# A hybrid retention/attention layer with a gated MLP: the up-projection by Strassen's algorithm, the output projection by token halves, and the late stages in program order

## The chip, the cores and the metric

The kernel runs on one core of one Trainium2 chip, in one launch. The metric is the device time of the whole launch in microseconds. The kernel before was timed three times: 2539.72 us median (2537.1 to 2542.47).

## The reference

One decoder layer for 1024 tokens plus 16 meta tokens, width 1024, all float32. What matters here is its second half:

```python
ro  = (silu(rg) * groupnorm(ro)) @ w_ret_o            # 2048 -> 1024
do  = rmsnorm(do, diff_subln_w) @ w_diff_o            # 1024 -> 1024
mix = (sigmoid(g_ret) * ro + sigmoid(g_diff) * do) @ w_out
h   = h + mix
u   = rmsnorm(h, norm2_w)
up  = causal_dwconv(u @ w_up, conv_w, conv_b)         # 1024 -> 2 * 2816, 3 taps
a, b = split(up, 2)
h   = h + (silu(a) * b) @ w_down                      # 2816 -> 1024
```

## The kernel before

Activations lie channel by channel: a tile has 128 channels on the partitions and up to 1040 tokens along its rows. Every float32 factor of a matmul is split into a high part (a cast to fp32r, on ScalarE) and a low part (source minus high part, on VectorE or GpSimd), and each product is three matmuls: high by high, high by low, low by high. So each block of 128 by 128 weights costs three matmuls for each group of tokens, and a group is 342 tokens (`QG`: three groups) or 512 (the down-projection: two).

**Stages.** Phase 1 projects the normed input (`w_in`) and runs differential attention; phase 2 runs the retention of four heads, with the output projection of one head (`ret_out`, w_ret_o) mixed into the next head's retention; the last head's `ret_out` stands alone at the end of phase 2, and beside it `load_head` and `norm_head` bring in and scale the eight attention heads. Phase 3 is `w_diff_o` (8 output tiles), the gated merge with the retention, `w_out` (8 output tiles, each 8 blocks by 3 groups by 3 matmuls) and the residual with its RMS norm. Phase 4 is the MLP: 22 steps f; each step makes two output tiles of the up-projection (f and 22 + f; `up`, L1190) of 8 blocks by 3 groups by 3 matmuls, the convolution (`conv`, L1205), silu and the product (L1247 and L1248) and the split of the result (L1250). After every second step, `down` (L1215) adds the share of two such tiles to all 8 output tiles, 96 matmuls of 512 tokens. The up-projection thus has 44 x 8 x 3 x 3 = 3168 matmuls of 342 tokens, the down-projection 11 x 96 = 1056 of 512.

**What sets the order.** Parts of phases 1 and 2 stand in `manual_schedule` (program order); the rest, and all of phases 3 and 4, are put in order by the tile framework's scheduler. Weights come in one list, `stream`: `next_w` (L213) takes a block that is loaded, and `load_w` (L232) issues the two halves of the next on SP's DMA queue, casts them on ScalarE (L229) and takes the low parts on GpSimd (L230). All matmuls but transposes are recorded on L176. One set of pools (`cst`, `big` with 34 tiles of 1040 tokens, `w`, `tmp`, `ps`) serves the whole kernel; the eight PSUM banks are 2 `acc`, 4 `sc`, 1 `st` and 1 `ot`.

Of the kernel before, what the change touches and what calls it, by code (L numbers as in the profile page):

```python
# [10 lines left out]
F32 = mybir.dt.float32  # L11
# [86 lines left out]
class Builder:  # L98
    ATT_WEIGHT, RET_WEIGHT = 38.666666666666664, 27.0

    def __init__(self, ctx, tc, a, chunk_dec):
# [5 lines left out]
        self.cp = pool("cst")  # L107
        self.bp = pool("big", 34)
        self.wp = pool("w", 2)
        self.tp = pool("tmp", 2)  # L110
        self.ps = pool("ps", 2, space=PSUM)
        self.dr = pool("dr", 1, space=DRAM)
        self.n = 0
# [199 lines left out]
    def setup(self):  # L313
# [7 lines left out]
        pc = cp.tile([P, a["cols"].shape[1]], F32, name="cols")  # L321
# [6 lines left out]
        qkw = cp.tile([P, 3], F32, name="qkw")  # L328
# [15 lines left out]
    def const_cast(self):  # L344
        a, cp, S, A = self.a, self.cp, self.S, self.A
        c, craw, nr = self.c, self.craw, C_KD - C_Z6
        cr = cp.tile([P, nr], F32R, name="constsr")
# [473 lines left out]
    def phase1(self):  # L821
# [18 lines left out]
        order = []  # L840
        for n in range(0, NF, 2):
            down = [a["w_down"][n - 2], a["w_down"][n - 1]] if n else []
            up = [a["w_up"][f] for f in (n, NF + n, n + 1, NF + n + 1)]
            order += up[:2] + down + up[2:] if n < NF - 2 else up + down
        order += [a["w_down"][NF - 2], a["w_down"][NF - 1]]
# [184 lines left out]
    def ret_out(self, h):  # L1030
        last = h == RH - 1
        order = [(m, g) for m in range(8) for g in range(3)]
# [3 lines left out]
        for m, g in order:  # L1036
# [3 lines left out]
            if h == 0 and g == 0:  # L1040
                self.racc.append(self.big())
            ps = self.acc6() if last else self.acc()
# [10 lines left out]
    def phase2(self, rest, nrest):  # L1053
        self.gh, self.gl = {}, {}
        self.racc = []
        prev, units = rest, nrest
        for h in range(RH):
            self.blend(self.retention(h), self.RET_WEIGHT, prev, units)
            prev, units = self.ret_out(h), 24
        self.heads = []  # L1060
        for _ in range(4):
            next(prev)
        self.ret_tail()
        with self.tc.manual_schedule():
            coming = [self.load_head(0)]
            for i, _ in enumerate(prev):
                if i % 3 == 0 and i < 20:
                    coming.append(self.load_head(i // 3 + 1))
                elif i % 3 == 2:
                    self.norm_head(i // 3, *coming.pop(0))  # L1070
            while coming:
                self.norm_head(len(self.heads), *coming.pop(0))
# [13 lines left out]
    def norm_head(self, h, d, y):  # L1086
# [3 lines left out]
        self.split(a[:, q], b[:, q], d[:, q])  # L1090
        self.heads.append((a, b))


    def phase3(self):
        V, A, G, S = self.V, self.A, self.G, self.S
        q = slice(HALO, T)
        dh, dl = ([t[i] for t in self.heads] for i in range(2))
        self.heads = None
        gates = {}

        def gate(kind, m):
            t = self.big()
            S.dma_start(out=t[:, q], in_=self.spill[kind, m][:, q])
            A.activation(t[:, q], t[:, q], AF.Sigmoid)
            return t

        gates.update({(k, 0): gate(k, 0) for k in ("gr", "gd")})
        for m in range(8):
            w = self.next_w()
            gr, gd = gates.pop(("gr", m)), gates.pop(("gd", m))  # L1110
            if m < 7:
                gates.update({(k, m + 1): gate(k, m + 1) for k in ("gr", "gd")})
            mx = self.racc[m]
            G.tensor_mul(mx[:, q], mx[:, q], gr[:, q])
            for t0, n in QG:
                ps = self.acc6()
                for _ in self.bulk(ps[:, :n], [((w[0][:, k, :], w[1][:, k, :]), (dh[k][:, t0:t0 + n], dl[k][:, t0:t0 + n])) for k in range(8)]):
                    pass
                cs = slice(t0, t0 + n)
                V.tensor_mul(gd[:, cs], ps[:, :n], gd[:, cs])  # L1120
                V.tensor_add(mx[:, cs], mx[:, cs], gd[:, cs])
                self.tick()
        mh, ml = [], []
        for m in range(8):
            a, b = self.big(F32R), self.big(F32R)
            self.split(a[:, q], b[:, q], self.racc[m][:, q])
            mh.append(a)
            ml.append(b)
        self.h = []
        self.vh2, self.vl2 = [], []  # L1130
        sq = self.big()

        def normed(m):
            a, b = self.big(F32R), self.big(F32R)
            self.split(a[:, q], b[:, q], self.h[m][:, q], scale=self.n2[m])
            self.vh2.append(a)
            self.vl2.append(b)

        def finish(m, g, ps):
            t0, n = QG[g]  # L1140
            h = self.h[m][:, t0:t0 + n]
            V.tensor_add(h, h, ps[:, :n])
            s = sq[:, t0:t0 + n]
            if m == 0:
                A.activation(s, h, AF.Square)
            else:
                x = self.tmp("sq", bufs=2)
                A.activation(x[:, :n], h, AF.Square)
                G.tensor_add(s, s, x[:, :n])  # L1149
            if m == 7 and g == 2:  # L1150
                sh, sl = self.big(F32R), self.big(F32R)
                self.split(sh[:, q], sl[:, q], sq[:, q])

                def stat():
                    st = self.st()
# [157 lines left out]
```

## Time and profile before

| | |
|---|---|
| median of 3 runs | 2539.72 us (2537.1 to 2542.47) |
| the profiled execution, its own time | 2539.37 us |
| span of its instructions | 2537.6 us |
| mean granted TensorE clock | 0.997 |
| TensorE busy | 2497.5 us, 98% of the span, 15444 matmuls |
| VectorE, ScalarE, GpSimd busy | 1597.8, 908.0 and 607.6 us |
| DMA | 224.55 MB, mean 88 GB/s |

The span runs from the first to the last instruction; the execution's own time is 1.8 us longer. Matmuls are pipelined: the trace shows each with a duration, but the next starts before it has ended, so what one matmul costs in a stream is read from the starts, or from a stretch that holds a known number of them. In the trace a line is that of the helper that records the instruction; stages are told apart by time and by tile names. The last head's `ret_out` begins at about 1555 us, `w_diff_o` at about 1603, `w_out` at about 1697, the up-projection at about 1788.

### The profile page before, as it was taken

The numbers are of one execution on the slowest core, as the hardware profiler recorded it, in microseconds if no ns is written. First come the engines' busy times: TensorE is split into PE (matmuls) and PEld (weight loads), VectorE is DVE, ScalarE is ACT, GpSimd is POOL, SyncE is SP. The second block draws the span as 40 slices with busy tenths as digits, with TensorE's granted clock in tenths as the row PEclk, the third lists the DMA queues.
The fourth block names the chain that finished last, engine by engine and source line by source line (L and its number), as shares of the span: only waits on it lengthen the run. The fifth ranks groups of instructions, "written<-read, shape, count | busy, mean of one in ns | idle before, by whom it ended". The sixth has DMA issues, their size and how long they took to land. (4 is left out here: it accounts for less than half of the span.)

```text
span 2537.6 us, 40442 instructions
## 1 busy us (share of the span) xinstructions
PE 2497.5 (98%) x15444; PEld 2407.4 (95%) x15444; DVE 1597.8 (63%) x3382; ACT 908.0 (36%) x1883; POOL 607.6 (24%) x495
## 2 busy tenths in 40 slices
PE   8999999999999999999999999999999999999999
PEld 8899999999999999999998999999999999999998
DVE  7665757576565757554888887642656556655555
ACT  5343525344343435344566563423311111111111
POOL 1301010101011010101333432525323333333332
PEclk9999999999999999999999999999999999999999
DMA  4524242424242242424443443513111111111112
GB/s 167 131 79 119 77 118 75 111 64 111 73 106 90 81 117 72 119 75 130 115 110 94 104 107 122 208 59 101 46 46 51 43 49 51 42 50 48 45 50 87
DMA packets 171538, 224.55 MB, mean 88 GB/s; under 512 B 26713, under 2 KB 109265, under 8 KB 171345
## 3 DMA queue, kind: packets, MB, share of 16 engines
q1 hardware_dynamic: 165440, 202.70, 26.2%
q0 software_dynamic: 5760, 19.17, 3.7%
q8 instruction: 121, 1.98, 0.3%
q14 instruction: 73, 0.59, 0.1%
q10 hardware_dynamic: 144, 0.10, 0.0%
HBM read 160.20 MB, written 42.35 MB: 80 GB/s over the span
## 5 line engine op out<-in xcount | busy, mean ns | idle before, releaser
L176 PE MATMUL acc<-b,wh 128*128 128x342 f32 (+3 forms) x5948 | 1444.8, 325 | 15.3 <-DVE b L430 8.9
L176 PEld LDWEIGHTS acc<-b,wh 128*128 128x128 f32 x5948 | 1028.7, 189 | 27.7 <-issue 8.8
L176 PE MATMUL acc<-b,wl 128*128 128x342 f32 (+3 forms) x2974 | 964.0, 324 | 1.5 <-POOL wl L230 1.5
L176 PE MATMUL sc<-b,wh 128*128 128x342 f32 (+2 forms) x2580 | 647.7, 334 | 1.1 <-ACT b L242 1.1
L176 PEld LDWEIGHTS acc<-b,wl 128*128 128x128 f32 x2974 | 561.3, 189 | 7.7 <-POOL wl L230 2.6
L176 PEld LDWEIGHTS sc<-b,wh 128*128 128x128 f32 x2580 | 455.4, 189 | 22.4 <-ACT b L242 1.4
L230 POOL TENSOR_TENSOR wl<-wr,wh 128x512 fp32r<-128x512 f32 x212 | 297.4, 1423 | 608.6 <-ACT wh L229 608.4
L176 PE MATMUL sc<-b,wl 128*128 128x342 f32 (+2 forms) x1290 | 429.7, 334 | 0.0
L229 ACT CAST wh<-wr 128x512 fp32r<-128x512 f32 x366 | 213.0, 619 | 594.4 <-PE acc L176 249.8
L176 PEld LDWEIGHTS sc<-b,wl 128*128 128x128 f32 x1290 | 243.5, 189 | 10.0
L247 POOL TENSOR_TENSOR b<-b,b 128x512 fp32r<-128x512 f32 (+1 forms) x86 | 137.8, 1602 | 342.4 <-ACT b L242 317.1
L607 DVE TENSOR_TENSOR ev<-acc,b 128x342 f32<-128x342 f32 (+1 forms) x144 | 74.0, 514 | 171.4 <-PE acc L176 165.5
L242 ACT CAST b<-b 128x512 fp32r<-128x512 f32 (+3 forms) x137 | 102.2, 750 | 217.2 <-DVE b L1248 146.7
L1211 DVE SCALAR_TENSOR_TENSOR b<-b,cols,b 128x1024 f32<-128x1024 f32 x88 | 148.6, 1688 | 2.3
L696 ACT ACTIVATE b<-b,sm 128x272 f32<-128x272 f32 (+7 forms) x128 | 101.2, 790 | 107.6 <-DVE sm L695 84.2
L688 DVE CUSTOM_DVE_ANT_0 b<-sc,consts 128x144 f32<-128x144 f32 (+6 forms) x224 | 105.9, 504 | 41.0 <-PE sc L176 40.0
L1202 DVE TENSOR_TENSOR b<-sc,b 128x342 f32<-128x342 f32 x84 | 42.5, 511 | 139.1 <-PE sc L176 139.1
L573 POOL TENSOR_TENSOR sh<-sh,b 128x346 f32<-128x346 f32 (+1 forms) x42 | 43.1, 1026 | 358.7 <-DVE sh L571 358.7
L230 DVE TENSOR_TENSOR wl<-wr,wh 128x512 fp32r<-128x512 f32 x154 | 107.3, 714 | 22.1 <-ACT wh L229 22.0
L242 ACT CAST ah<-sc 128x512 fp32r<-128x512 f32 (+2 forms) x144 | 67.3, 467 | 118.0 <-PE sc L713 92.8
L1226 DVE TENSOR_TENSOR b<-b,sc 128x512 f32<-128x512 f32 x117 | 78.7, 683 | 48.3 <-PE sc L176 48.3
L247 DVE TENSOR_TENSOR al<-sc,ah 128x512 fp32r<-128x512 f32 (+2 forms) x144 | 77.4, 538 | 43.2 <-ACT ah L242 42.1
(249 smaller groups left out, 2748.5 us busy)
## 6 DMA issues: line engine op xcount, KB each, us to landing
wr<-w_in SPq DMA_DIRECT2D x170, 256.0 KB
wr<-w_up SPq DMA_DIRECT2D x88, 256.0 KB
d<-ev SPq DMA_DIRECT2D x120, 171.0 KB
b<-b POOLq DMA_DIRECT2D x72, 260.0 KB, 4.6
b<-d SPq DMA_DIRECT2D x256, 64.0 KB
b<-d SPq DMA_DIRECT2D x24, 513.0 KB
wr<-w_down SPq DMA_DIRECT2D x44, 256.0 KB
b<-d SPq DMA_DIRECT2D x32, 260.0 KB
```

The lines of the kernel that those rows point to most:

```text
L176: self.E.matmul(out, lhsT=l, rhs=r, start=start, stop=stop)
L229: self.A.copy(h, raw)
L230: (self.G if el == "G" else self.V).tensor_sub(l, raw, h.bitcast(F32))
L242: self.A.copy(dh, src)
L247: (self.V if el == "V" else self.G).tensor_sub(dl, src, dh.bitcast(F32))
L573: G.tensor_mul(sh[:, :n], sh[:, :n], self.Sn[:, cs])
L607: V.tensor_mul(o[:, :n], ps[:, :n], self.rb[:, cs])
L688: V.tensor_tensor_reduce(out=sc_[:m, a0:a0 + sz], in0=ps[:m, :sz], in1=mk, scale=1.0, scalar=3e38, op0=ALU.add, op1=ALU.min, accum_out=sm[ ...
L696: A.activation(sc_[:m, :n], sc_[:m, :n], AF.Exp, bias=mx, scale=-1.0, accum_out=sm[:m, 10 + c:11 + c])
L1202: self.V.tensor_mul(up[:, t0:t0 + n], ps[:, :n], self.rb2[:, t0:t0 + n])
L1211: V.scalar_tensor_tensor(out=o[:, q], in0=up[:, NMETA - 2 + i:T - 2 + i], scalar=self.cw(i, fi), in1=o[:, q], op0=ALU.mult, op1=ALU.add)
L1226: self.V.tensor_add(h, h, ps)
```

## The change

**Pools.** Constants that are needed to the end move to a pool `keep`. After the first half of the last `ret_out` (output tiles 0 to 3), `back()` closes the other pools but `big` and opens new ones in their memory: 10 tiles each for high and low weights of half a block (128x512), 8 raw tiles, and PSUM as 3 double banks and 2 single ones, later (after the first half of `w_out`) as 4 double banks. Everything from there on is in program order.

**Late part of phase 2 and phase 3.** `ret_out` of output tiles 4 to 7 and `w_diff_o` are computed with the three groups of 342 side by side under each weight tile. The norms of the heads are spread from the last `ret_out` into the first 2 output tiles of `w_diff_o`. `w_out` is computed twice over, first the tokens of one half for all 8 output tiles (2 x 256 columns), then the other half (2 x 258), with its weights loaded and split twice: 8 x 8 x 3 x 4 = 768 matmuls. While the second half runs, the first half's residual is stored to DRAM, normed, and turned into the operands of the up-projection.

**Up-projection.** For each f, the two output tiles, the two token halves of 516 and the two halves of the 1024 input channels form a 2 x 2 by 2 x 2 product. It is computed with 7 products instead of 8 (Winograd's form of Strassen's algorithm), named A, B, E, F, H, G and D in the code; each has 4 blocks by 3 matmuls by 2 pieces of 258 columns, 24 matmuls. The five token operands that are sums or differences are made once, on VectorE. Of the weights of each f, four sums are needed: two (s1, s3) are made by DMAs on GpSimd's queue that add a second block from DRAM to a raw tile already loaded, and two (S, T) by VectorE. The 4 PSUM results that have to be combined are added up by VectorE into `sw`, `su` and two output tiles of 1032 columns. A and B of f = 0 to 3 are computed ahead, in the last part of phase 3. In all 22 x 7 x 24 = 3696 matmuls of 258 columns.

**Convolution and down-projection.** The first tap is a ScalarE instruction with scale and bias, the other two are VectorE's, in halves of 512. They run one step behind. The product goes to DRAM, and the whole down-projection (again 1056 matmuls of 512) follows after the last up-projection, reading it back two tiles at a time.

```diff
-        self.stream = ([a["w_in"][b] for _, _, b in seq] + [a["w_ret_o"][i] for i in range(16)]
-                       + [a["w_diff_o"][i] for i in range(8)] + [a["w_out"][i] for i in range(8)] + order)
+        self.stream = [a["w_in"][b] for _, _, b in seq] + [a["w_ret_o"][i] for i in range(14)]
...
+    def product(self, outs, pairs, start=True, stop=True, more=False):
+        last = len(pairs) - 1
+        for i, ((wh, wl), (xh, xl)) in enumerate(pairs):
+            for l, x, f, e in ((wh, xh, start and i == 0, False), (wh, xl, False, False), (wl, xh, False, stop and i == last)):
+                for o, t0, n in outs:
+                    self.E.matmul(o[:, :n], lhsT=l, rhs=x[:, t0:t0 + n], start=f, stop=e, skip_group_check=more)
...
+    HALF = [[(12, 256), (268, 256)], [(524, 258), (782, 258)]]
+    PIECES = [(0, 258), (258, 258)]
...
+        pss = [self.dbl() for _ in ws]
+        for k in range(8):
+            for w, ps in zip(ws, pss):
+                self.product(outs(ps, 0), [(w(k), x(k))], k == 0, k == 7)
+        for m, ps in enumerate(pss):
+            finish(m, 0, ps)
+        for m in range(3, 8):
...
+            finish(m, 0, ps)
+        self.ps_early.close()
...
+        for m in range(8):
+            w = self.block(1)
+            ps = self.dbl()
+            self.product(outs(ps, 1), [(w(k), x(k)) for k in range(8)])
...
+        self.first("A", 0)
+        add_square()
+        self.pre_weights(3)
+        squares(1)
...
+        self.first("A", 1)
+        self.weights(0, "F")
+        stat()
...
+    def operand_f(self, *ks):
+        for k in ks:
+            self.scaled(4 + k, 1)
+            self.V.tensor_add(self.half(k, 0), self.half(4 + k, 1), self.half(k, 0))
+            self.put("F", k, self.half(k, 0))
+            self.lows(1)
...
+    def quad_loads(self, f, names="s1 s3 a b d"):
...
+            r[n] = self.raw_quarter(src[n][0][:, src[n][1], :])
+    def sum_d(self, f, *names):
+        r = self.raws[f]
+        for n in names or ("s1", "s3"):
+            src = self.a["w_up"][NF + f][:, 4:, :] if n == "s1" else self.a["w_up"][f][:, :4, :]
+            self.nc.gpsimd.dma_start(out=r[n], in_=src, accum_op=ALU.add)
+    def weights(self, f, names):
+        q, r = self.wq.setdefault(f, {}), self.raws[f]
+        for n in names:
+            if n == "S":
+                self.V.tensor_add(r["a"], r["a"], r["s1"])
+            elif n == "T":
+                self.V.tensor_add(r["b"], r["b"], r["a"])
+            else:
+                q[n] = self.split_w(r[dict(A="a", B="b", F="a", H="s3", E="s1", G="d", D="b")[n]], "G" if n in self.pooled else "V")
+    def quad_product(self, ps, f, name, more=False):
+        w = self.wq[f].pop(name)
+        outs = [(ps[:, 512 * g:512 * g + 512], t0, n) for g, (t0, n) in enumerate(self.PIECES)]
+        self.product(outs, [((w[0][:, k, :], w[1][:, k, :]), self.xs(name, k)) for k in range(4)], not more, True, more)
...
+        for f in range(2, NF):
...
+                self.quad_product(pt, f, "A")
+                A.copy(bd(st[f]), d2(pt))
+                w()
+                taps(1)
...
+            up_f(f)
...
+            w()
+            if not pro:
+                taps(0)
+                self.quad_product(pt, f, "B", True)
+                A.copy(bd(ua[f][:, :516]), d2(pt))
+                w()
...
+                self.quad_loads(f + 2)
+            up_e(f)
...
+            up_h(f)
+            mid(f)
...
+            mul()
...
+                self.sum_d(f + 2)
...
+            up_g(f)
...
+            up_d(f)
...
+        for p in range(NF // 2):
+            gh, gl = down
...
+                self.product([(ps[:, :512], 0, 512), (ps[:, 512:], 512, 512)], [(w(o + i), (gh[i], gl[i])) for i in range(2)])
...
 def hybrid_layer(ctx: ExitStack, tc: tile.TileContext, a: dict, chunk_dec):
     b = Builder(ctx, tc, a, chunk_dec)
-    b.phase2(*b.phase1())
-    b.phase3()
-    b.phase4()
+    prev = b.phase2(*b.phase1())
+    with tc.manual_schedule():
+        b.last_ret_out(prev, ctx)
+        b.phase3()
+        b.phase4()
```

`w()` stands for: take all low parts that are due on VectorE, then prepare the next of the weights of f + 1, in the order A, S and F, B, H, E, T and G, D. The low parts of B, E and D are GpSimd's, those of A, F, H and G VectorE's.

**How it moves instructions.** On TensorE, in the middle of the up-projection, the kernel before takes one group of 342 tokens through the 8 blocks of an output tile (`acc` is the PSUM tile, `b` the token operand, `wh` and `wl` the weights):

```order
L176 MATMUL acc_23375<-b_19566,wh_23272 128x342
L176 MATMUL acc_23375<-b_19567,wh_23272 128x342
L176 MATMUL acc_23375<-b_19566,wl_23273 128x342
L176 MATMUL acc_23375<-b_19669,wh_23272 128x342
L176 MATMUL acc_23375<-b_19670,wh_23272 128x342
L176 MATMUL acc_23375<-b_19669,wl_23273 128x342
```

and the changed kernel two pieces of 258 under each weight tile, here at the end of H and the start of G of one f:

```order
L1165 MATMUL d_23467<-b_20923,wh_23251 128x258 x2
L1165 MATMUL d_23467<-b_20924,wh_23251 128x258 x2
L1165 MATMUL d_23467<-b_20923,wl_23252 128x258 x2
L1165 MATMUL d_23511<-b_21004,wh_23296 128x258 x2
L1165 MATMUL d_23511<-b_21005,wh_23296 128x258 x2
L1165 MATMUL d_23511<-b_21004,wl_23297 128x258 x2
```

The matmuls are narrower, and of each weight tile two follow each other.

VectorE in the same stage of the kernel before, for one output tile and the start of the next (L1202 reads PSUM, L1209 and L1211 are the convolution, L1226 adds the down-projection's result):

```order
L1226 TENSOR_TENSOR b_20079<-b_20079,sc_24136 128x512
L1202 TENSOR_TENSOR b_24179<-sc_24154,b_20192 128x342
L1202 TENSOR_TENSOR b_24179<-acc_24181,b_20192 128x342
L1202 TENSOR_TENSOR b_24179<-acc_24207,b_20192 128x342
L1209 TENSOR_SCALAR b_24233<-b_24179,cols 128x1024
L1211 SCALAR_TENSOR_TENSOR b_24233<-b_24179,cols,b_24233 128x1024 x2
L1202 TENSOR_TENSOR b_24272<-sc_24247,b_20192 128x342
```

and of the changed kernel, from F of one f to the taps of the next (`d` are PSUM tiles, `wr` raw weights, `wl` low parts; L1535 and L1537 are S and T, L1579 taps, L1584 the product with silu, L1604 to L1624 what is read from PSUM):

```order
L1604 TENSOR_TENSOR sw_23146<-u_23087,d_23121 128x516
L1117 TENSOR_TENSOR wl_23115<-wr_22946,wh_23114 128x512
L1535 TENSOR_TENSOR wr_22946<-wr_22946,wr_22942 128x512
L1579 SCALAR_TENSOR_TENSOR b_23079<-u_22597,cols,b_23079 128x512 x4
L1117 TENSOR_TENSOR wl_23151<-wr_22946,wh_23150 128x512
L1610 TENSOR_TENSOR su_23247<-d_23222,sw_23146 128x516
L1614 TENSOR_TENSOR b_23249<-su_23247,d_23197 128x516
L1584 TENSOR_TENSOR b_23079<-b_23079,b_23047 128x512 x2
L1117 TENSOR_TENSOR wl_23252<-wr_22944,wh_23251 128x512
L1619 TENSOR_TENSOR b_23249<-d_23266,su_23247 128x516
L1537 TENSOR_TENSOR wr_22948<-wr_22948,wr_22946 128x512
L1624 TENSOR_TENSOR u_23087<-sw_23146,d_23197 128x516
```

With one more low part and four more taps this is the whole round of one f, 21 instructions; weight sums, low parts and taps stand between the reads of PSUM.

GpSimd in the same stage before (L230 are low parts of weights, L247 that of the result)

```order
L247 TENSOR_TENSOR b_25589<-b_25489,b_25588 128x1024
L230 TENSOR_TENSOR wl_25686<-wr_25687,wh_25685 128x512
L230 TENSOR_TENSOR wl_25686<-wr_25691,wh_25685 128x512
L230 TENSOR_TENSOR wl_25785<-wr_25786,wh_25784 128x512
L230 TENSOR_TENSOR wl_25785<-wr_25790,wh_25784 128x512
```

and now (the DMA rows are the adding transfers s1 and s3, the others low parts):

```order
L1123 TENSOR_TENSOR wl_22449<-wr_22213,wh_22448 128x512
L1528 DMA wr_22452<-w_up 128x512
L1528 DMA wr_22454<-w_up 128x512
L1123 TENSOR_TENSOR wl_22528<-wr_22207,wh_22527 128x512
L1123 TENSOR_TENSOR wl_22594<-wr_22213,wh_22593 128x512
```

Where the queue held low parts alone, it now holds three of them and two transfers for each f, which wait in it for their raw tiles.

## Rows read from the trace of the kernel before

**Rows 1.** The page: busy time of each engine; granted clock in 40 slices.
```profile
PE 2497.5 (98%) x15444; PEld 2407.4 (95%) x15444; DVE 1597.8 (63%) x3382; ACT 908.0 (36%) x1883; POOL 607.6 (24%) x495
...
PEclk9999999999999999999999999999999999999999
```

**Rows 2.** Stretches: us, busy PE, PEld, DVE, ACT, POOL (count), clock, DMA, GB/s.
```profile
1560.00:1611.00 51.00, 50.45 (x319) 50.19 (x319) 30.02 (x39) 12.71 (x19) 10.19 (x8) 1.00 0.49 164
1611.00:1614.00 3.00, 0.44 (x4) 0.29 (x3) 1.59 (x2) 1.05 (x1) 0.00 (x0) 1.00 1.03 412
1614.00:1618.00 4.00, 4.00 (x19) 3.98 (x19) 0.92 (x1) 1.27 (x3) 0.60 (x1) 0.65 0.77 312
1618.00:1640.00 22.00, 22.00 (x141) 22.00 (x140) 17.95 (x18) 14.26 (x17) 19.75 (x11) 0.99 0.62 216
...
1812.00:2533.00 721.00, 720.82 (x4077) 674.90 (x4076) 430.69 (x458) 119.48 (x171) 237.03 (x150) 1.00 0.16 51
```

**Rows 3.** The chain that ended last: start, us, engine, tile, line, count.
```profile
2244.78 15.13 PE sc L176 x96
...
2289.71 7.58 PE acc L176 x48
...
2507.48 5.57 PE sc L176 x24
```

**Rows 4.** Timeline of PE in attention: start us, us, operation; six 256-column matmuls.
```profile
181.27 0.28 PE L176 MATMUL ot<-al,vh 128*128 128x256 f32 x1
181.39 0.28 PE L176 MATMUL ot<-ah,vl 128*128 128x256 f32 x1
...
181.87 0.48 PE L176 MATMUL acc<-b,wh 128*128 128x348 f32 x2
```

**Rows 5.** The page's costliest groups: weight loads, busy us, mean ns.
```profile
L176 PEld LDWEIGHTS acc<-b,wh 128*128 128x128 f32 x5948 | 1028.7, 189 | 27.7 <-issue 8.8
```

**Rows 6.** Timeline of PE at two waits, at 1611 and at 1788 us.
```profile
1610.84 0.31 PE L176 MATMUL sc<-b,wh 128*128 128x342 f32 x1
1613.71 0.42 PE L176 MATMUL acc<-b,wh 128*128 128x342 f32 x1 [2.56 <-ACT b L242]
...
1615.57 0.49 PE L176 MATMUL sc<-b,wh 128*128 128x342 f32 x1
1615.85 0.49 PE L176 MATMUL sc<-b,wl 128*128 128x342 f32 x1
...
1787.58 0.47 PE L176 MATMUL acc<-b,wh 128*128 128x342 f32 x2
1789.70 0.42 PE L176 MATMUL st<-b,constsr 128*128 128x342 f32 x1 [1.66 <-ACT b L242]
```

**Rows 7.** Groups of DVE by line and shape: busy us, mean ns, idle before.
```profile
L1211 DVE SCALAR_TENSOR_TENSOR b<-b,cols,b 128x1024 f32<-128x1024 f32 x88 | 148.6, 1688 | 2.3
L1226 DVE TENSOR_TENSOR b<-b,sc 128x512 f32<-128x512 f32 x117 | 78.7, 683 | 48.3 <-PE sc L176 48.3
L1248 DVE TENSOR_TENSOR b<-b,b 128x1024 f32<-128x1024 f32 x22 | 26.8, 1220 | 1.3
L230 DVE TENSOR_TENSOR wl<-wr,wh 128x512 fp32r<-128x512 f32 x154 | 107.3, 714 | 22.1 <-ACT wh L229 22.0
```

**Rows 8.** The same for ACT and POOL.
```profile
L229 ACT CAST wh<-wr 128x512 fp32r<-128x512 f32 x174 | 99.5, 618 | 396.1 <-issue 196.0 <-PE sc L176 112.5 <-PE acc L176 83.7
L1247 ACT ACTIVATE b<-b 128x1024 f32<-128x1024 f32 x22 | 23.3, 1061 | 106.7 <-DVE b L1211 106.7
L230 POOL TENSOR_TENSOR wl<-wr,wh 128x512 fp32r<-128x512 f32 x174 | 247.7, 1445 | 498.7 <-ACT wh L229 498.7
```

**Rows 9.** One line's instructions: DMAs on GpSimd's queue (L645, attention).
```profile
L645 POOL DMA_DIRECT2D b<-b x24: 512/526/582, 85.1 to 1030.4; - x24
...
DMA to landing us min/median/max: 2.9/4.7/7.9
```

More of the change, by code (lines that the diff above doesn't have):

```diff
@@ L1031, in ret_out @@
         last = h == RH - 1
-        order = [(m, g) for m in range(8) for g in range(3)]
+        order = [(m, g) for m in range(4 if last else 8) for g in range(3)]
         if last:
@@ L1063, in phase2 @@
         self.ret_tail()
[L1064 to L1072, printed above, removed]
+        return prev
     def load_head(self, h):
@@ L1089, in norm_head, with back @@
         a, b = self.big(F32R), self.big(F32R)
-        self.split(a[:, q], b[:, q], d[:, q])
+        self.A.copy(a[:, q], d[:, q])
+        self.low_later(b[:, q], d[:, q], a[:, q])
         self.heads.append((a, b))
+    def back(self, ctx):
+        self.flush()
+        self.front.close()
+        tc, a = self.tc, self.a
+        pool = lambda n, b=1, **k: ctx.enter_context(tc.tile_pool(name=n, bufs=b, **k))
+        self.tp = pool("tmp2", 1)
+        self.wp = pool("w2", 10)
+        self.ps_early = ExitStack()
+        self.ps = self.ps_early.enter_context(tc.tile_pool(name="ps2", bufs=1, space=PSUM))
+        self.queue = [a["w_diff_o"][i] for i in range(8)] + 2 * [a["w_out"][i] for i in range(8)]
+        self.coming, self.ready, self.low = [], [], "V"
+        self.acts = []
+        self.request()
+        self.request()
@@ new lines, in quarter, with raw_quarter, low_later, lows @@
+    def quarter(self):
+        return tuple(self.wp.tile([P, 4, P], F32R, tag=t, name=self.nm(t)) for t in ("wh", "wl"))
+    def raw_quarter(self, src):
+        raw = self.wp.tile([P, 4, P], F32, tag="wr", name=self.nm("wr"), bufs=8)
+        if src is not None:
+            self.S.dma_start(out=raw, in_=src)
+        return raw
+    def low_later(self, l, x, h):
+        self.late.append((l, x, h))
+    def lows(self, keep=0):
+        while len(self.late) > keep:
+            l, x, h = self.late.pop(0)
+            self.V.tensor_sub(l, x, h.bitcast(F32))
@@ new lines, in block, with dbl, sng, pair @@
+    def block(self, level=1):
+        w = self.ready.pop(0)
+        while len(self.ready) < level and self.coming:
+            self.arrive()
+            self.request()
+        return lambda k: tuple(t[:, k % 4, :] for t in w[k // 4])
+    def dbl(self):
+        return self.ps.tile([P, 1024], F32, tag="d", name=self.nm("d"), bufs=self.doubles)
+    def sng(self): return self.ps.tile([P, 512], F32, tag="s", name=self.nm("s"), bufs=2)
+    @staticmethod
+    def pair(ps, n):
+        return ps.rearrange("p (a b) -> p a b", a=2)[:, :, :n]
@@ new lines, in triple, with like @@
+    def triple(self):
+        d, s = self.dbl(), self.sng()
+        banks = [d[:, :512], d[:, 512:], s]
+        outs = [(o, t0, n) for o, (t0, n) in zip(banks, QG)]
+        reads = [(slice(14, 698), self.pair(d, 342)), (slice(698, 1040), s[:, :342])]
+        return outs, reads
+    @staticmethod
+    def like(t, cs):
+        v = t[:, cs]
+        return v.rearrange("p (a b) -> p a b", a=2) if cs.stop - cs.start == 684 else v
+    HALF = [[(12, 256), (268, 256)], [(524, 258), (782, 258)]]
@@ L1096, in phase3 @@
         q = slice(HALO, T)
-        dh, dl = ([t[i] for t in self.heads] for i in range(2))
-        self.heads = None
+        norm, load = self.more
+        self.lows()
         gates = {}
```

617 lines of the change are left out of this document (472 added, 145 removed).

## The prediction

> **What bounds the kernel now.** First the page: TensorE is busy for 98% of the span at full clock [rows 1], so time goes only with work or waits of TensorE. Then the stretches: from 1812 to 2533 us it is busy for 720.82 of 721 us, and VectorE, the next, for 430.69 [rows 2]: in the MLP nothing but matmul time counts. What a matmul costs in a stream comes from the chain: 96 of 342 columns in 15.13 us are 157.6 ns each, 48 in 7.58 us 157.9, and 24 of 512 in 5.57 us 232.1 [rows 3]; I take 157.7. Between the two lie 170 columns and 74.4 ns, 0.438 ns a column: 2.3 columns per ns, nearly the upper level of the clock (2.4 GHz), plus some 8 ns for each matmul. So columns count, and instructions hardly do. Last the waits: in what the change rewrites, from 1555 us on, TensorE waits at 1611 us for the last head (next start 2.87 us after the last) and then runs for some 4 us at a granted clock of 0.65, with starts 0.28 us apart; at 1788 us it waits for the statistics (1789.70 less 1787.58 us, for two matmuls) [rows 2, 6]. Above the pace that is 2.7 us, 1.0 (19 matmuls in 4.00 us, which would take 3.0) and 1.8; with shorter gaps elsewhere I put the waits there at 8 to 12 us and take 10.
>
> **The change, part by part.** The sum is made against the profiled execution's own time, 2539.37 us (span 2537.6); the median, 2539.72 us, lies 0.35 us above, which I neglect.
>
> *Up-projection, matmuls.* Removed: 3168 x 157.7 ns = 499.6 us. Added: 3696 of 258 columns. By the two widths of rows 3, 157.7 - 84 x 0.438 = 120.9 ns. Six matmuls of 256 columns in attention start 0.12 us apart (five steps, 0.60 us) [rows 4], so two more columns give 121 as well. Both are other widths or short runs, so I keep 118 and 125 as bounds (-11 and +15 us). Added: 447.2 us. Saved: 52.4 us, 2.38 us for each f.
>
> A rule speaks against it. The Trainium skill, "TensorE: Matmul & The Clock Gate", section "Back-to-back issue gap", says that in a stream of weight loads and matmuls the spacing follows from both, and gives 81 ns at 128 columns and 131 at 512. By a straight line between these (an estimate from that page) 342 columns would cost 108.9 ns and 258 97.9, and the up-projection would go from 345 to 362 us: 17 us slower, since the 528 extra matmuls cost more than the columns save. The trace disagrees: its 512 columns take 232 ns, so the measured price decides.
>
> *Second projection.* 576 x 157.7 = 90.8 us become 768 of 256 or 258 columns, 92.7 us: +1.9. The last `ret_out`, w_diff_o and the down-projection keep their matmuls: 0.
>
> *VectorE in the loop.* For each f: 5 reads of PSUM at 683 ns, 4 low parts and 2 weight sums at 714, 8 taps at half of 1688, 2 products at half of 1220 [rows 7]: 3.4 + 4.3 + 6.8 + 1.2 = 15.7 us, against 7 x 24 x 0.121 = 20.3 us of TensorE. The order matters too. After H, VectorE has su, a difference, two products, one low part, then waits for G: 3.3 us, G takes 2.9. Sum T and the result of D follow, ending 6.5 us after H; F of the next f, the first to need D's banks, starts 8.7 us after H. So 2 us are left where it is tightest: 0.
>
> *ScalarE and GpSimd.* ScalarE: 7 casts at 618 ns, 6 passes over 512 columns of about the same, silu 1.06 us: 9.1 us. GpSimd: 3 low parts at 1445 ns and 2 issues at 526 ns: 5.4 us [rows 8, 9]. All in 20.3 us: 0.
>
> *The adding DMAs.* No row shows one. The nearest are copies on the same queue, 260 KB in 2.9 to 7.9 us, median 4.7 [rows 9]; reading the destination as well may double that, 15.8 at worst. For f + 2 they are issued during f, behind the low part of B: 0.6 + 0.6 + 1.4 us after B ends, plus 1.1 us for two issues. S needs the sum after F of f + 1, six products or 17.4 us after B. So 13.7 us are left: I take twice the median, 9.4 us, fully covered: 0 (bounds 0 and (15.8 - 13.7) x 18 = 38 us).
>
> *DMA queues and traffic.* On SP's queue each f has 5 loads and, behind them, the store of a result, which waits for the products; so the loads for f + 3 can start no earlier than some 2.6 us after H of f, a whole step before they are needed. Each f moves 7 blocks of 256 KB and 512 KB of results in 20.3 us, some 116 GB/s. TensorE stayed fully busy at 216, while 412 fills the engines [rows 2]. 0.
>
> *Extra down-projection traffic, last step.* The whole down-projection at the end has 22.3 us of matmuls for each pair; VectorE needs 16 halves at 683 ns and some 5 us of low parts. 0; the end itself, with both halves of the last tile ending together, +0.7 us.
>
> *Waits that go.* The last head is now needed 8 steps deep in a loop over two tiles, and the statistics are run half by half: the 10 us go.
>
> *Waits that come.* Program order has four seams, none of them in the trace. (1) At `back()` and at the second PSUM change, the new banks wait for the last reads, each about one read of 0.7 us: 1.5. (2) Six heads now have to pass VectorE in about 38 us of TensorE, with reads of `ret_out` queued behind each wait for a head; that stretch already moved 164 GB/s and ended at 412 [rows 2]: 0 to 6, I take 2. (3) Before the second half's statistics VectorE waits for two sums of s1; behind it stand squares, some nine steps of a reciprocal root and the scaling. TensorE has 8 products of A and B, 23 us, to fill: 0 to 6, I take 2. (4) E, F, H and G operands cost VectorE 8 + 8 + 5 + 5 us at about 0.69 us a step, the PSUM reads 5 more, against 35 us of products; the fourth part of G comes some 2 us late, and f = 2 and 3, with only 14.5 us of products, wait 2 more: 4, up to 12. With the end: 10 us, bounds 3 and 30.
>
> **Sum.** 2539.4 - 52.4 + 1.9 - 10 + 10 + about 1 for retention steps that the scheduler orders differently = **2490 us**, 1.9% faster.
>
> **Rivals.** About 0.2%, 5 us, is what a measurement can tell from no change.
>
> *A lag in each step.* If one queue in the loop comes 1 us late for each f (VectorE's low parts slowed by GpSimd, ScalarE's casts behind silu), 22 us come back: 2512. For it: VectorE's 77% load and mixed order; against it: the 2 us left above. 0.13.
>
> *The seams take all.* Waits at the seams of 45 to 55 us: 2535 to 2540. It needs several waits over 10 us, while the trace's longest here is 2.7. 0.04.
>
> *The adding DMAs come late (slower).* S stands on VectorE ahead of the taps and of the read of H, so a late sum stops TensorE in every step. It decides from 13.7 us on, and costs 18 us for each further us: at 18 us of landing 2490 + 77 = 2567. For it: nothing in the trace adds in a DMA, and DVE and SP queues wait behind. Against: 4.7 us for a copy. 0.05.
>
> *The weight load sets the pace of a narrow matmul (slower).* A load lasts 189 ns [rows 5], longer than 121, and each matmul has its own. If loads cannot be overlapped in long runs of 258 columns, 4464 matmuls cost 68 ns more each: 2490 + 304 = 2794. It decides from 135 ns on (499.6 us by 3696). Against it: rows 4, six in a row at 120. 0.03. The page named above has this rule in milder numbers, its 17 us more.
>
> **How the numbers follow.** My forecast has 0.75, the lag 0.13, the rest as given. The forecast's own bounds: low, 118 ns and few waits: 2490 - 13 = 2477, I say 2478; high, 125 ns or waits of 30: 2510. The lag reaches 2522. So 2478 to 2522 holds 0.88 less its own tails, about 0.8. Faster by over 0.2%: 0.75 + 0.13 = 0.88; same: 0.04; slower: 0.05 + 0.03 = 0.08.
>
> **What would show it.** Right: matmuls of 258 columns start 121 ns apart, f = 4 to 21 take 20.3 us each with TensorE busy without gaps, VectorE waits there mainly for TensorE, and the waits left lie between `back()` and f = 3. Wrong: a pace of over 125 ns; TensorE waiting in every f, for VectorE (low parts) or through S for a DMA; a drop of the granted clock at the seams.

## The result, and the profile after

The changed kernel takes **2498.26 us** (median of 4 runs, 2497.32 to 2499.06). The kernel before took 2540.18 us beside it (4 runs, 2537.1 to 2542.47): a ratio of 0.9836, 95% interval 0.9819 to 0.9853, 42 us less. The forecast was 2490, 8 us too low. The profiled execution took 2498.22 us, with a span of 2496.4 us.

The page's first part answers to [rows 1]: TensorE is busy for 51 us less, and still for 98% of the span.

```profile
PE 2446.9 (98%) x16168; PEld 2352.7 (94%) x16168; DVE 1704.9 (68%) x3625; ACT 1041.4 (42%) x2106; POOL 430.3 (17%) x412
```

The same stage can be compared in both traces from one mark on, the end of a short pause of TensorE on ScalarE near the end of the retention. The timeline of the kernel before has it at

```profile
1560.55 0.75 PE L176 MATMUL sc<-b,wh 128*128 128x342 f32 x2 [1.11 <-ACT b L242]
```

and that of the changed kernel at

```profile
1556.45 0.75 PE L180 MATMUL sc<-b,wh 128*128 128x342 f32 x2 [1.11 <-ACT b L246]
```

From there to the end of the span the kernel before takes 977.0 us (2537.6 - 1560.55) and the changed one 939.9 (2496.4 - 1556.45): **37.1 us less**, where the forecast's terms for this part come to 50.5 (52.4 - 1.9 + 10 - 10). Ahead of the mark lie another 4.1 us. In the twelve other profiles of this document, whose kernels differ from the changed one only behind this mark, it falls between 1553.52 and 1558.57 us. That is a spread of 5 us by itself, so what is compared below is the part behind the mark.

The table of stretches of the changed kernel (busy time by engine, instructions in brackets, then granted clock, DMA share and GB/s) answers to [rows 2] and shows where TensorE is not busy:

```profile
1555.00:1790.00 235.00, 229.40 (x1645) 227.06 (x1642) 137.96 (x182) 84.55 (x126) 19.61 (x14) 1.00 0.49 162
1790.00:1815.00 25.00, 24.24 (x197) 23.78 (x197) 23.20 (x41) 8.76 (x17) 1.74 (x2) 1.00 0.30 75
1815.00:1890.00 75.00, 67.22 (x516) 64.29 (x515) 65.45 (x82) 33.64 (x54) 36.03 (x27) 0.98 0.45 120
1890.00:2250.00 360.00, 360.00 (x2968) 359.13 (x2967) 261.11 (x368) 159.17 (x249) 96.50 (x85) 1.00 0.44 117
2250.00:2496.00 246.00, 240.06 (x1037) 194.31 (x1035) 166.60 (x178) 48.01 (x66) 0.00 (x0) 1.00 0.33 118
```

In the loop, 1890 to 2250 us, nothing is missing: 360.00 of 360, 2968 matmuls, 121.3 ns each (a few matmuls may be missing from the records). Its step is read from silu, once in each f, on ScalarE's timeline: 20.27 us.

```profile
2014.11 1.06 ACT L1582 ACTIVATE b<-b 128x1024 f32<-128x1024 f32 x1 [1.43 <-DVE b L1579]
2034.38 1.06 ACT L1582 ACTIVATE b<-b 128x1024 f32<-128x1024 f32 x1 [1.43 <-DVE b L1579]
```

Since 20.27 us by 168 matmuls are 120.7 ns, the price of 120.9 was right. The idle time lies at the seams, above all from 1815 to 1890 us (7.8 us). TensorE's waits from 1550 us on, by what ended them (us in total, times, longest):

```profile
PE d L1165 <- DVE b L1117: 5.2, 6, 2.0
PE d L1165 <- ACT u L1695: 2.0, 1, 2.0
PE d L1165 <- DVE b L1047: 1.7, 1, 1.7
PE d L1165 <- POOL wl L1123: 1.4, 3, 0.6
...
PE d L180 <- ACT b L246: 0.9, 1, 0.9
PE d L1165 <- DVE b L1321: 0.9, 1, 0.9
PE d L1165 <- DVE b L1614: 0.8, 1, 0.8
```

On the timeline the four long ones are `back()`, the operands of G, the copy of the first product of f = 4 and the last pair of tiles of the down-projection:

```profile
1573.61 0.55 PE L1165 MATMUL d<-b,b 128*128 128x342 f32 x2 [1.72 <-DVE b L1047]
...
1834.30 0.51 PE L1165 MATMUL d<-b,wh 128*128 128x258 f32 x2 [1.48 <-DVE b L1117]
...
1884.74 0.80 PE L1165 MATMUL d<-b,wh 128*128 128x258 f32 x2 [2.01 <-ACT u L1695]
...
2469.88 0.73 PE L1165 MATMUL d<-b,wh 128*128 128x512 f32 x2 [1.98 <-DVE b L1117]
```

Last, the page's table of DMA issues (KB each, median us to landing) has the operation that no row of before showed. An adding DMA lands as fast as the copies of [rows 9], whose median is 4.7 us too:

```profile
wr<-w_up POOLq DMA_DIRECT2D x44, 256.0 KB, 4.7
```

### The profile page after: what moved, and what is told of

Read it like the earlier page. It is cut to its first block, busy times and chain, and to the rows that moved or that the text cites. A ratio compares the mean times of both kernels' runs of the same rounds, so it can differ in the third digit from the quotient of the medians.

```text
span 2496.4 us, 42738 instructions
## 1 busy us (share of the span) xinstructions
PE 2446.9 (98%) x16168; PEld 2352.7 (94%) x16168; DVE 1704.9 (68%) x3625; ACT 1041.4 (42%) x2106; POOL 430.3 (17%) x412
## 5 line engine op out<-in xcount | busy, mean ns | idle before, releaser
L180 PE MATMUL acc<-b,wh 128*128 128x342 f32 (+2 forms) x4720 | 1132.6, 323 | 13.7 <-DVE b L434 9.5
L180 PEld LDWEIGHTS acc<-b,wh 128*128 128x128 f32 x4720 | 810.9, 189 | 15.7 <-issue 9.5
L180 PE MATMUL acc<-b,wl 128*128 128x342 f32 (+2 forms) x2360 | 756.9, 321 | 1.0 <-POOL wl L234 1.0
L1165 PE MATMUL d<-b,wh 128*128 128x258 f32 (+3 forms) x3936 | 734.9, 306 | 9.3 <-DVE b L1117 5.2
L1165 PEld LDWEIGHTS d<-b,wh 128*128 128x128 f32 x3936 | 587.7, 189 | 42.9 <-DVE b L1117 6.9
L180 PEld LDWEIGHTS acc<-b,wl 128*128 128x128 f32 x2360 | 445.6, 189 | 1.6 <-POOL wl L234 1.6
L1165 PE MATMUL d<-b,wl 128*128 128x258 f32 (+3 forms) x1968 | 441.6, 306 | 2.3 <-POOL wl L1123 1.4
L1165 PEld LDWEIGHTS d<-b,wl 128*128 128x128 f32 x1968 | 319.3, 189 | 19.1 <-POOL wl L1123 2.5
L1123 POOL TENSOR_TENSOR wl<-wr,wh 128x512 fp32r<-128x512 f32 x84 | 116.2, 1400 | 511.1 <-ACT wh L1121 497.1
L1766 DVE TENSOR_TENSOR b<-b,d 128x1024 f32<-128x1024 f32 (+1 forms) x96 | 107.3, 1129 | 76.6 <-PE d L1165 73.6
```

The lines of the kernel that those rows point to most:

```text
L180: self.E.matmul(out, lhsT=l, rhs=r, start=start, stop=stop)
L1123: self.G.tensor_sub(w[1], raw, w[0].bitcast(F32))
L1165: self.E.matmul(o[:, :n], lhsT=l, rhs=x[:, t0:t0 + n], start=f, stop=e, skip_group_check=more)
L1766: V.tensor_add(h[m][:, cs], h[m][:, cs], ps[:, cs])
```

## The experiments

All are edits of the changed kernel, on one core. Runs without an interval are one execution each.

### An eighth product

```diff
-        self.product(outs, pairs, not more, True, more)
+        for _ in range(2 if name == "G" and f >= self.PRO else 1):
+            self.product(outs, pairs, not more, True, more)
```

> Eight products instead of seven: in f = 4 to 21 the 24 matmuls of product G are issued twice, the second time from the start, so the result stays the same. Theory (TensorE sets each step and a matmul of 258 columns costs 121 ns): 18 x 24 x 0.121 = 52 us more than the changed kernel's 2498, so 2550, and the step goes from 20.3 to 23.2 us. Rival (a step is as long as some other queue makes it, TensorE only looks busy): well under 52, say below 30, so under 2530.

Measured: 2549.83 us, 51.6 us more; silu comes every 23.15 us:

```profile
2007.98 1.06 ACT L1583 ACTIVATE b<-b 128x1024 f32<-128x1024 f32 x1 [1.43 <-DVE b L1580]
2031.13 1.06 ACT L1583 ACTIVATE b<-b 128x1024 f32<-128x1024 f32 x1 [1.43 <-DVE b L1580]
```

That is 2.88 us for 24 matmuls, 120 ns each. Between seven and eight products every matmul costs its full price: the seven products, not the program order, give the gain of the loop. With eight products of 258 columns the up-projection would cost 4224 x 0.1207 = 510 us, more than the 499.6 before.

### Half as wide

```diff
+        if f >= self.PRO and name in "FHG":
+            for j in range(2):
+                self.product([(o[:, 128 * j:], t0 + 128 * j, (128, 130)[j]) for o, t0, n in outs], pairs)
+            return
```

> Products F, H and G of f = 4 to 21 are computed in two passes of 128 and 130 columns for each bank: 48 matmuls of about 129 columns instead of 24 of 258, with the same columns in all and the same result. Theory (0.438 ns a column and 8 ns for each matmul): 64.5 ns each, 54 products x (48 x 64.5 - 24 x 121) = +10 us, 2508. Rival (below some width the weight load sets the pace): at 109 ns a matmul +126 us, 2624; at the 81 ns that the Trainium skill, TensorE: Matmul & The Clock Gate, section Back-to-back issue gap, gives for 128 columns, +54 us, 2552.

Measured: 2625.18 us, 127 us more than the changed kernel. The theory falls; the rival's 109 ns is close. The step is 27.62 us:

```profile
2000.55 1.06 ACT L1587 ACTIVATE b<-b 128x1024 f32<-128x1024 f32 x1 [1.43 <-DVE b L1584]
2028.17 1.06 ACT L1587 ACTIVATE b<-b 128x1024 f32<-128x1024 f32 x1 [1.43 <-DVE b L1584]
```

Less 96 matmuls of 258 columns at 120.7 ns this leaves 16.03 us for 144 narrow ones, 111 ns each. Half the columns save only 10 ns. TensorE does not wait for another engine there (360.00 of 360 us busy, from 1890 to 2250 us):

```profile
1890.00:2250.00 360.00, 360.00 (x3130) 360.00 (x3129) 198.22 (x277) 117.57 (x185) 75.83 (x68) 1.00 0.33 86
```

So the straight line of the prediction (0.438 ns a column and 8 ns), which holds at 258, 342 and 512 columns, does not go on to 130. Drawn on, it would meet the floor at (111 - 8) / 0.438 = 235 columns, an estimate: no experiment has a width between 130 and 256. The forecast's 258 lay just above it.

Each of these matmuls has a weight load of its own, and no run took the load away. But the trace of the kernel before speaks for the load as the cause: on its timeline in attention, matmuls of 128 columns follow wider ones (PEld is the weight loads):

```profile
135.26 0.19 PEld L176 LDWEIGHTS ot<-ah,vh 128*128 128x128 f32 x1
135.37 0.22 PE L176 MATMUL ot<-ah,vh 128*128 128x128 f32 x1
135.37 0.19 PEld L176 LDWEIGHTS ot<-al,vh 128*128 128x128 f32 x1
135.43 0.28 PE L176 MATMUL ot<-al,vh 128*128 128x128 f32 x1
135.48 0.19 PEld L176 LDWEIGHTS ot<-ah,vl 128*128 128x128 f32 x1
135.54 0.27 PE L176 MATMUL ot<-ah,vl 128*128 128x128 f32 x1
```

The first is followed after 0.06 us, which is what the line gives for 128 columns (64 ns); the second only after 0.11 us, and 0.11 us is the distance of the loads. The 81 ns that the Trainium skill gives for 128 columns (TensorE: Matmul & The Clock Gate, Back-to-back issue gap) is not seen here: 111.

### More additions: two, three, four for each weight sum

```diff
-        for n in names or ("s1", "s3"):
+        for n in names or 2 * ("s1", "s3"):
```

(and 4 and 3 in the place of the 2)

> Each weight sum of f = 2 to 21 is added twice by DMA, in the order s1, s3, s1, s3; the second adding waits for the first, on GpSimd's queue. This changes the sums, so s1 and s3 hold a block too much. In the changed kernel the issue of s1 lies 16.4 us before the sum S that needs it (2013.47 and 2029.87 us in the trace). Theory (the adding DMA is covered): the sums land after about 11.5 us instead of 5.6, GpSimd's queue is held for some 7 us in each step, and the time stays at 2498 within 3 us. Rival (the sums are only just in time): up to 5.6 us for each of 18 to 20 steps, 2600.

> As the run with two additions, but four for each sum (the sums are again not those of the layer). Theory (covered up to the slack of 16.4 us, then each us late costs a us in each step): four additions end after some 22.4 us, 6.0 too late, and GpSimd's queue with its three low parts is held for 22.5 us of a step of 20.3: 2.2 to 6 us in each of 18 to 20 steps, 2540 to 2620, and TensorE waits in each step through S on VectorE. Rival (adding DMAs and late sums never matter, since TensorE has enough finished weights): 2498.

> As the run with two additions, but three for each sum. Two cost nothing that could be told, four cost 115 us. From the four: 20.6 us from the first issue (2008.03) to S (2028.64), 5.2 for each addition. Theory (free up to a slack of some 16.4 us): three need 15.5 us and are just covered, GpSimd's queue is held for some 14 of 20.3 us: 2500, at most 2515. Rival (the cost grows with each addition from the second on): half of the way to four, some 2555.

Measured: two 2500.04 us (ratio to the kernel before 0.9845, 0.9822 to 0.9867; the changed kernel 0.9836), no difference that can be told. Four 2613.31, 115 us more. Three 2518.84: 21 us more. The cost of three lies at the start, not in the loop; its stretches are

```profile
1850.00:1905.00 55.00, 38.88 (x287) 38.25 (x287) 32.96 (x41) 17.30 (x26) 28.01 (x27) 0.88 0.75 146
1905.00:2250.00 345.00, 344.64 (x2840) 344.01 (x2839) 280.67 (x359) 149.43 (x237) 154.21 (x147) 1.00 0.75 164
```

TensorE is idle for 16 us while f = 2 to 4 have no lead, with a granted clock of 0.88 in that stretch, and then for 0.4 of 345 us. So the slack was about as large as computed, and the theory missed the start. Four show what a late sum does, first on GpSimd's timeline:

```profile
2008.03 1.82 POOL L1528 DMA_DIRECT2D wr<-w_up  x2 [0.20 <-POOL wl L1123]
2012.50 0.88 POOL L1528 DMA_DIRECT2D wr<-w_up  x1 [2.65 <-DMA wr<-w_up]
...
2026.21 0.87 POOL L1528 DMA_DIRECT2D wr<-w_up  x1 [0.95 <-DMA wr<-w_up]
2026.78 2.82 POOL L1123 TENSOR_TENSOR wl<-wr,wh 128x512 fp32r<-128x512 f32 x2
```

Eight issues wait one for another, and the low part behind them starts 18.8 us after the first. TensorE waits for that low part, not, as expected, for S; its row, and the granted clock in the stretches around it:

```profile
2028.43 0.65 PE L1165 MATMUL d<-b,wl 128*128 128x258 f32 x2 [2.77 <-POOL wl L1123]
```

```profile
2025.80:2028.40 2.60, 0.00 (x0) 0.00 (x0) 0.00 (x0) 0.00 (x0) 2.19 (x3) 1.00 0.88 124
2028.40:2032.20 3.80, 3.77 (x18) 3.78 (x19) 3.53 (x4) 2.01 (x4) 1.50 (x2) 0.55 0.86 216
```

After a stop of some 3 us TensorE runs for 3.8 us at a granted clock of 0.55, little above the lower level of 1.2 GHz, and starts only 18 matmuls where 31 fit at 120.7 ns: 1.6 us on top of the wait.

### Low parts without GpSimd

In the loop alone, and then from the second half of `w_out` on (the second with this line too):

```diff
-            self.pooled = "EFHGD" if f + 1 < self.PRO else "BED"
+            self.pooled = "" if f >= self.PRO else "EFHGD" if f + 1 < self.PRO else "BED"
...
-            self.G.tensor_sub(w[1], raw, w[0].bitcast(F32))
+            self.V.tensor_sub(w[1], raw, w[0].bitcast(F32))
```

> From f = 4 on the three low parts of a step that GpSimd makes (B, E and D) are VectorE's; same result. In the changed kernel VectorE's instructions from SBUF to SBUF are longer while GpSimd runs one (512 columns 749 ns alone, 1214 ns with 635 ns of overlap, 34 of 139 between 1890 and 2250 us); those that read PSUM are not (690 and 694). Theory (covered: VectorE has 5.6 us left in each step of 20.3): 3 x 0.68 us more and some 0.9 less of stretching, 1.2 us more for each f, all covered: 2498 within 2 us. Rival (the order in a step leaves under 1 us at its tightest): 0.5 to 1 us for each of 17 steps, 2506 to 2515.

> As the run without GpSimd's low parts in the loop, and before it too: from the second half of w_out to f = 3 VectorE makes them directly behind each cast; same result. The question is what the seam from 1797 to 1846 us pays for sharing: VectorE works there without a pause for 40 us and TensorE waits some 7 us for its operands, while GpSimd runs 11 low parts. Theory (GpSimd's help costs VectorE there what it saves: 688 ns alone, 1422 with overlap): within 3 us of 2498. Rival (GpSimd really relieves VectorE): 11 x 0.68 = 7 us more in the seam, 2505.

Measured: in the loop alone 2496.1 us (ratio 0.984, 0.9826 to 0.9853), everywhere 2500.14 (0.9849, 0.9835 to 0.9862). Neither can be told from the changed kernel; from the mark on they take 939.3 and 940.9 us against 939.9. The taps show what sharing cost. From 1890 to 2250 us, by shape (xcount | busy us, mean ns), in the changed kernel

```profile
L1579 DVE SCALAR_TENSOR_TENSOR b<-u,cols,b 128x512 f32<-128x512 f32 x68 | 64.4, 967 | 1.2
...
L1624 DVE TENSOR_TENSOR u<-sw,d 128x516 f32<-128x516 f32 x18 | 12.5, 693 | 23.3 <-PE d L1165 23.3
```

and without GpSimd in the loop

```profile
L1579 DVE SCALAR_TENSOR_TENSOR b<-u,cols,b 128x512 f32<-128x512 f32 x67 | 48.8, 749 | 1.2
...
L1624 DVE TENSOR_TENSOR u<-sw,d 128x516 f32<-128x516 f32 x18 | 12.5, 693 | 2.9 <-PE d L1165 2.6
```

The group of taps of which about half meet a low part on GpSimd goes from 967 to 749 ns in the mean. The read of PSUM at L1624, which in the changed kernel lies within such a low part (2022.63 to 2023.33 us, GpSimd from 2022.06 to 2023.35, and so in nearly every f), stays at 693. One tap of the changed kernel shows what happens, on the timeline from 2012.37 us on:

```profile
2012.23 1.29 POOL L1123 TENSOR_TENSOR wl<-wr,wh 128x512 fp32r<-128x512 f32 x1 [9.15 <-ACT wh L1121]
2012.39 1.68 DVE L1579 SCALAR_TENSOR_TENSOR b<-u,cols,b 128x512 f32<-128x512 f32 x1
```

It begins while GpSimd is at work, and ends 0.55 us after GpSimd does: it seems to have stood still for most of the low part. In this loop GpSimd still takes more off VectorE than it costs: 261.11 us of 360 busy, against 277.73 without it.

### The next bound

```diff
-        for k in range(4)
+        for k in range(3 if f >= self.PRO else 4)
```

Then the same, with the line of the loop above that takes the low parts from GpSimd.

> In f = 4 to 21 every product takes three of its four blocks (18 matmuls of 24), so a quarter of the up-projection's sums is left out; all other work stays. Theory (TensorE alone sets the step, and the next queue, VectorE, needs some 14.5 us of it): 42 x 0.1205 = 5.1 us less for each f, the step 15.2 us, 91 us in all, 2407. Rival (the order in a step, with VectorE's waits for each product, is itself a limit close below 20 us): a step of 17 us or more, 2440 or above, and TensorE waits in each step.

> Three quarters of each product as before (a quarter of the up-projection's sums left out in f = 4 to 21), and from f = 4 on GpSimd's three low parts of a step are VectorE's. With GpSimd's help the step of the run before was 16.82 us, VectorE busy for 266.63 of 270 us, its mean instruction 789 ns against 709 in the changed kernel. Theory (VectorE is the next bound, and what GpSimd takes off it comes back as longer instructions): without the stretching VectorE needs some 15.6 us for each f (277.73 of 360 us in the run without GpSimd's low parts in the loop), so the step goes to 15.6 to 15.9 us, some 20 us less than 2436, 2416, though VectorE gets three more instructions. Rival (GpSimd does relieve VectorE): 3 x 0.61 = 1.8 us more for each f, 18.6 us, 2469.

Measured: 2436.27 us and **2415.89**. In the first, neither side had the step exactly (15.2 or 17 us): TensorE pauses once in each f, 16.82 us apart,

```profile
2012.64 0.75 PE L1165 MATMUL d<-b,wh 128*128 128x258 f32 x4 [1.42 <-DVE b L1614]
2029.46 0.75 PE L1165 MATMUL d<-b,wh 128*128 128x258 f32 x4 [1.42 <-DVE b L1614]
```

and VectorE, in the third busy column, is busy for 266.63 of 270 us, with 338 instructions:

```profile
1890.00:2160.00 270.00, 248.37 (x2035) 245.10 (x2034) 266.63 (x338) 141.98 (x227) 97.93 (x81) 1.00 0.53 138
```

Without GpSimd it does 411 in the same time, and the step is 15.68 us:

```profile
1890.00:2160.00 270.00, 265.71 (x2179) 262.44 (x2178) 266.39 (x411) 149.21 (x241) 30.99 (x34) 1.00 0.56 148
```

Where VectorE is the bound, three more instructions in each f make the step 1.1 us shorter: here GpSimd's help cost VectorE more than it took off it.

### The seams

The first edit takes the special case from the fetch and the split of the last pair (as at the others, tiles 0 and 3), and makes the last weights of f = 4 later. The second has the edits of the low parts as well.

```diff
-                if m == (4 if p == NF // 2 - 2 else 0) and not last:
+                if m == 0 and not last:
...
-                if m == (6 if p == NF // 2 - 2 else 3) and not last:
+                if m == 3 and not last:
...
                 A.copy(bd(st[f]), d2(pt))
+                for names in pending:
+                    self.weights(f, names)
+                pending = []
...
+            if pro and not f + 1 < self.PRO:
+                pending = list(todo)
```

> Two waits of the changed kernel taken away, same result: the last pair of tiles of the down-projection is fetched and split as early as the others (TensorE waits 2.1 us at 2467 us), and the last weights of f = 4 are made behind the copy of its first product instead of ahead of it (2.2 us at 1882 us, released by that copy on ScalarE). Theory (the miss of 8 us is such waits, and each is its own): 4.3 us less, 2494. Rival (the wait comes back at the next product): 2498.

> Both edits together: the two waits taken away, and all low parts from the second half of w_out on VectorE. Theory (they are independent): the sum of the two alone, 2491 to 2497. Rival (VectorE, now with all low parts, is late for the operands and gives the gain back): 2498 to 2505.

Measured: 2495.75 us (0.9834, 0.9821 to 0.9848) and 2493.42 (0.9831, 0.9818 to 0.9845), the lowest of all, but its interval still covers the changed kernel's 0.9836. From the mark on they take 936.6 and 935.9 us against 939.9, which is 3.3 and 4.0 less: the waits at 1884 and 2469 us are gone, and in the first 1.4 us came back some 15 us later, where TensorE waits for VectorE:

```profile
1899.01 0.36 PE L1165 MATMUL d<-b,wh 128*128 128x258 f32 x1 [1.39 <-DVE b L1614]
```

The last experiment asks for the cause of the waits from 1817 to 1834 us:

```diff
     def operand_e(self, *ks):
         for k in ks:
-            self.scaled(k, 1)
...
     def operand_f(self, *ks):
         for k in ks:
-            self.scaled(4 + k, 1)
```

> The eight scalings of the second half's operands (746 ns each on VectorE, between 1799 and 1815 us of the changed kernel) are left out, so that half of the MLP's input is not normed. It asks what TensorE waits for between 1817 and 1834 us, where its waits are 4.9 us. Theory (VectorE's queue, which works there for 40 us without a pause, is late as a whole): with 6 us less ahead of it these waits go nearly to 0, 4 to 5 us less from the last ret_out to the end than the 941.3 us of the changed kernel. Rival (the waits are the way from one operand's sum through its cast on ScalarE to its low part): they stay, 941.

Measured: 2496.78 us, and 939.9 us from the mark on, as before the edit (the 941.3 of the expectation counts the pause at the mark too). The theory falls. VectorE has 6 us less to do, but waits four times for a cast on ScalarE, 5.1 us in all (the first row below is one), and then stops in its own order, as its timeline shows:

```profile
1804.45 0.70 DVE L1117 TENSOR_TENSOR b<-b,b 128x516 fp32r<-128x516 f32 x1 [1.58 <-ACT b L1456]
...
1817.73 0.69 DVE L1602 TENSOR_TENSOR sw<-u,d 128x516 f32<-128x516 f32 x1 [1.40 <-PE d L1165]
...
1822.24 3.48 DVE L1489 TENSOR_TENSOR b<-b,b 128x516 f32<-128x516 f32 x2
```

The read of the first F stands ahead of the rest of the H operands and waits for TensorE; the operands of H and G behind it are late again, and two differences that meet GpSimd take 3.48 us (1.29 in the changed kernel). So it is not the total of VectorE's queue that sets these waits. The way through the cast, which the rival names, and the order on the queue both show in the rows, and no run separates them. Other orders were not tried.

## Why the prediction was right, and where it missed

**The loop: right.** Starts of 258 columns are 120.7 ns apart (forecast 121), the step 20.27 us (20.3), TensorE without a gap. The eighth product priced the term by itself. No queue was late in a step, so the rival of a lag did not come. The Trainium skill's figures (TensorE: Matmul & The Clock Gate, Back-to-back issue gap), which the prediction turned into 17 us more, did not hold here: by them 258 columns take an estimated 97.9 ns, where 120 were measured, and 128 take 81, where it was 111.

**VectorE, ScalarE, GpSimd and the DMAs at nothing: right in the loop.** VectorE is busy for 14.7 us of 20.27 (261.11 of 360), 1 us under the 15.7 forecast. But its spare time is smaller than the difference: with less TensorE work the step stops at 16.82 us, so it had 3.5 us to spare, not 5.6, since its instructions get longer while GpSimd runs. The adding DMA was taken at 9.4 us and lands in 4.7.

**The rival of late sums: right in kind, wrong in price.** It was to cost 18 us for each us above 13.7. The slack is larger: three additions are covered in the loop, by the 5.2 us of each an estimated 15.5 us. Beyond it the cost comes through GpSimd's queue, its low parts standing behind the waiting issues, and through the granted clock.

**The rival of the weight load** was put at 0.03 from six matmuls in a row [rows 4]. A floor is there, at 111 ns, and it is most likely the load's; 258 columns clear it by 10 ns. The trace of before had it in its matmuls of 128 columns, which the prediction did not look at.

**Waits that go: the right ones, but too large.** The wait for the last head is gone; what is left at the statistics, 0.9 us and two shorter ones, belongs to the waits that come. But of the 10 us only 5.5 were read from rows, and the rest, "shorter gaps elsewhere", is hardly there. From the mark to the end of the last matmul the stretches of the kernel before and of the changed one are

```profile
1560.55:2533.86 973.31, 968.59 (x5628) 920.12 (x5628) 546.65 (x600) 199.47 (x286) 332.61 (x219) 1.00 0.21 68
```

```profile
1556.45:2492.03 935.58, 920.58 (x6352) 868.47 (x6352) 651.95 (x842) 333.77 (x509) 153.88 (x128) 1.00 0.42 128
```

so TensorE was idle for 4.7 us before (973.31 - 968.59); with the 1.0 us of the lower clock some 4 us of the term are missing.

**Waits that come: mis-sized, this is the larger part of the miss.** Behind the mark the gain is 37.1 us instead of 50.5, 13.4 less. By the same two rows TensorE's idle time there went from 4.7 us to 15.0, where the forecast had it nearly unchanged (10 go, 9.3 come); 0.6 us more lie behind the last matmul (0.7 forecast). By seams: `back()` and the second PSUM change 1.7 and 0.9 us for 1.5; the passing of the heads 0.7 and the statistics 1.6 for 2 each; the operands up to f = 4 7.8 for 4; the last pair of the down-projection 2.0 for nothing. On top of it the granted clock fell once, behind the wait of 2.0 us at 1884 us:

```profile
1885.00:1890.00 5.00, 5.00 (x31) 5.00 (x32) 4.93 (x7) 0.30 (x2) 0.89 (x1) 0.68 0.88 294
```

That costs some 1.5 us, about what the fall at 1614 us cost before [rows 2], so it adds little to the difference. But a fall at a seam is one of the prediction's own signs of being wrong, and it had placed no wait at f = 4 or in the down-projection.

The other 2.5 of the 13.4 us lie in busy time, which fell by 48.0 us instead of 50.5. Part of it is the run-out of the last matmul ahead of each wait, which counts as busy: 2.87 us from start to start around an idle of 2.56 [rows 6], 0.15 us over the pace, which for some 15 more waits is an estimated 2 us.

The sum of loads that the term was made from cannot show what one queue waits for in order, as the run without scalings shows. Some 5 us of the other side came ahead of the mark, -4.1 for +1, where the spread between executions is as large; what part of that the change made stays open. 13.4 less 5.1 are the 8 us of the miss: that it is 8 and not 13 rests on those 5 us, of which the prediction foresaw nothing, and so on luck.

## What to carry to other kernels

Where TensorE is busy for all of a stage, count columns, and price a matmul from rows of at least two widths; but look for the floor before making it narrower, here 111 ns at 128 and 130 columns. A DMA that adds cost no more here than one that copies, and its result was wanted only 16 us later; count what stands behind it on its issuing queue too. At the seams, go through each queue in order: an operand behind a read that waits is late however short the queue's work.

## What the runs showed of the hardware

**GpSimd lengthens VectorE's instructions on SBUF** that begin while it is at work. A tap of 512 columns takes 749 ns alone, and one that began inside a low part of GpSimd 1.68 us; the group of taps that partly meets GpSimd has a mean of 967. A read of PSUM that lies within a low part stays at 693, and a low part of VectorE's that had begun first took its 0.68 us, while GpSimd's took 1.57 instead of 1.29 (at 2000.27 and 2000.54 us in the run of three quarters). At VectorE's bound this is worth 1.1 us of a step of 16.8. The Trainium skill, Advanced Engine Details and Errata, section Mode Summary, says that VectorE's second SBUF port is shared with GpSimd, and that GpSimd's instructions and VectorE's two-port ("2p") instructions block each other. The trace agrees in that either one was held up by the other that had begun first, and shows it for float32 instructions with two inputs in SBUF; whether these count as two-port instructions no run shows.

**A floor of 111 ns** between matmuls of 128 or 130 columns with their own weights, at full granted clock; where the weights had been loaded ahead, the distance was 0.06 us.

**The adding DMA** of 256 KB: 4.7 us to landing, 5.2 in a chain (four from 2008.03 to S at 2028.64 us).
